# Four seven-product pairs instead of three in eight gate and up blocks, with the lo parts of three chunks per block made by an adding DMA

## The chip, the cores and the metric

The kernel runs on one NeuronCore of a Trainium2 chip. The metric is the device time of one execution, in microseconds (us). Before the change it is 1479.21 us, the median of three runs (1479.01 to 1479.62).

## The reference

One decoder layer on 256 tokens of width 2048, float32: a mixer, an attention over 256 memory tokens, a SwiGLU feed-forward part of width 5632, each behind an RMSNorm and added to the residual, and a last RMSNorm.

```python
h = x
h = h + hybrid_mixer(rmsnorm(h, norm_mix), w_in, ..., w_out)
h = h + memory_cross_attention(rmsnorm(h, norm_xa), mem_n, w_q, w_k, w_v, w_o)
h = h + swiglu(rmsnorm(h, norm_ffn), w_gate, w_up, w_down)
return rmsnorm(h, norm_final)

def swiglu(h, w_gate, w_up, w_down):
    return (jax.nn.silu(h @ w_gate) * (h @ w_up)) @ w_down
```

The change touches the two products `h @ w_gate` and `h @ w_up`.

## The kernel before, in words

**Chunks.** All weights stream from memory once, in one order (stream_plan). A chunk is 256 rows by 512 columns of a weight, held as one raw tile `r` of 128 partitions by 1024 elements (512 KB). SyncE (SP) issues the loads (load_to, L192 to L201) into six raw buffers, some five chunks ahead. The order of the work of TensorE (PE) and of SP is that in which the code is written (manual_schedule); the framework's scheduler orders VectorE (DVE), ScalarE (ACT) and GpSimd (POOL), and an engine runs its instructions strictly in that order.

**Hi and lo parts.** A float32 product is made of three products of a shorter format: hi with hi, lo with hi, hi with lo. split_to (L224) makes a chunk's hi part `h` by a cast on ACT (L238) and its lo part `l = r - h` on DVE (L239); there are four buffers for each. The activations are split in the same way beforehand. tok_mm (L303) multiplies a plain chunk by both halves of the tokens: eight matmuls with `h` (L312 hi, L313 lo of the activations), then four with `l` (L316), twelve in all.

**Gate and up blocks.** The feed-forward part goes by blocks n = 0 to 10 of 512 columns. In a block the chunks are (g,n,c) of the gate and (u,n,c) of the up weight, c = 0 to 7; below, g4 or u7 is c = 4 or 7 of the block that is spoken of. A gate and an up chunk of the same c may be made a pair (Strassen's method in Winograd's form, over two token halves and the two weights): 21 matmuls by seven_mm (L980; L990 and L991 with hi parts, L993 with lo parts) instead of the 24 of two plain chunks. A pair needs sums of its two chunks: pair_sums (L207) adds four times on DVE (L213 to L216), casts three sums on ACT (L220) and makes their lo parts on DVE (L221). The sums' parts lie in "slots" (63 buffers of 128 by 512). The matching sums of the activations come from token_sums (L954), once for each c. SEVEN (L31) says how many pairs each block has: three in blocks 1 to 9, two in block 10, none in block 0. Within a block with three pairs the order is pair 0, g3 g4 u3, pair 1, g5 u4 g6, pair 2, g7 u5 u6 u7.

**After a block.** What the pairs share is added up by p_post (L934, L938 to L942). `whole` (L1227, L1232) adds it to the accumulators of gate and up, on DVE, once the last matmul of these has run; g_post makes the silu (ACT, L1241), u_post the product (DVE, L1249). The result is transposed (DVE, L331), written to memory (SP, put, L344) and read back (SP, get, L351) in the layout for the down product, and split (L1259, L1260).

**Order around a block's start.** When the last matmul of u7 has run, PE goes on with pair 0 of the next block at once. DVE then has the old block's two `whole` of up (L1232), two L1249, two transposes, and then lo parts and the sums of the new block's pair 1. unit (L380) runs up to two parts after another, asks for loads up to AHEAD (6) chunks on and for splits one to three chunks on. A load waits until its raw buffer's last reader is done.

## Time and profile before

| | |
|---|---|
| median of three runs | 1479.21 us (1479.01 to 1479.62) |
| the profiled execution | 1479.07 us |
| its span in the profile | 1477.3 us |
| granted TensorE clock, mean | 0.999 |
| busy: PE, DVE, ACT, POOL | 1466.2, 1212.1, 864.2, 34.6 us |
| moved by DMA | 350.91 MB, mean 238 GB/s |

A profile is one execution, read by an engine's rows: the line of the program, the operation, the tiles written and read (`out<-in`, buffer numbers left out), the count, busy time and mean time of one in ns, and idle time of the engine ahead of the group with what ended it. Times of single instructions are microseconds from the start of the span. Instructions of an engine overlap a little, so that the step from one start to the next is shorter than the duration of one. The time of a run is about 1.8 us more than the span.

### The profile page before, as it was taken

The numbers are of one execution on the slowest core, as the hardware profiler recorded it, in microseconds if no ns is written. First come the engines' busy times: TensorE is split into PE (matmuls) and PEld (weight loads), VectorE is DVE, ScalarE is ACT, GpSimd is POOL, SyncE is SP. The second block draws the span as 40 slices with busy tenths as digits, with TensorE's granted clock in tenths as the row PEclk, the third lists the DMA queues.
The fourth block names the chain that finished last, engine by engine and source line by source line (L and its number), as shares of the span: only waits on it lengthen the run. The fifth ranks groups of instructions, "written<-read, shape, count | busy, mean of one in ns | idle before, by whom it ended". The sixth has DMA issues, their size and how long they took to land.

```text
span 1477.3 us, 18842 instructions
## 1 busy us (share of the span) xinstructions
PE 1466.2 (99%) x6592; PEld 1208.1 (82%) x6592; DVE 1212.1 (82%) x1738; ACT 864.2 (58%) x1228; POOL 34.6 (2%) x46
## 2 busy tenths in 40 slices
PE   9999999999999999999999999999999999999997
PEld 7788888888888888888888888888888887888886
DVE  6667777876786775897578999999999998979995
ACT  7467654866664544665466665556655554655663
POOL 0012000101000000000000000000000000000000
PEclk9999999999999999999999999999999999999999
DMA  9877766868667675777658766656676666765553
GB/s 367 273 252 260 264 220 228 289 219 307 228 240 267 198 249 186 254 271 278 226 172 296 263 217 230 214 212 228 229 248 248 206 237 229 269 219 199 195 202 112
DMA packets 151519, 350.91 MB, mean 238 GB/s; under 512 B 11616, under 2 KB 63232, under 8 KB 151424
## 3 DMA queue, kind: packets, MB, share of 16 engines
q1 hardware_dynamic: 142368, 342.83, 66.6%
q10 hardware_dynamic: 9056, 6.87, 1.6%
q8 instruction: 51, 0.84, 0.2%
q14 instruction: 44, 0.36, 0.1%
HBM read 323.40 MB, written 26.26 MB: 237 GB/s over the span
## 4 chain that ended last, share of the span: by engine, by line
PE 98%; DVE 1%; issue 0%; DMA 0%; ACT 0%; DVEq 0%; POOLq 0%; POOL 0%; SPq 0%
PE a L312 27%; PE a L313 26%; PE a L316 26%; PE m L993 3%; PE m L990 3%; PE m L991 3%; PE a L991 2%; PE a L990 2%; PE a L993 2%; PE m L733 1%; PE m L312 0%; PE m L313 0%; PE m L316 0%; PE m L1147 0%; PE m L735 0%
## 5 line engine op out<-in xcount | busy, mean ns | idle before, releaser
L238 ACT CAST h<-r 128x1024 fp32r<-128x1024 f32 (+1 forms) x539 | 562.5, 1048 | 405.2 <-PE a L313 231.8
L239 DVE TENSOR_TENSOR l<-r,h 128x1024 fp32r<-128x1024 f32 (+1 forms) x539 | 650.5, 1216 | 175.0 <-ACT h L238 166.5
L312 PE MATMUL a<-h,s 128*128 128x512 f32 x1735 | 679.3, 392 | 0.1
L313 PE MATMUL a<-h,s 128*128 128x512 f32 x1735 | 675.6, 389 | 0.0
L316 PE MATMUL a<-l,s 128*128 128x512 f32 x1735 | 466.9, 389 | 0.0
L312 PEld LDWEIGHTS a<-h,s 128*128 128x128 f32 x1735 | 326.0, 188 | 69.5 <-issue 2.0
L316 PEld LDWEIGHTS a<-l,s 128*128 128x128 f32 x1735 | 325.6, 188 | 68.1 <-DVE l L239 0.4
L313 PEld LDWEIGHTS a<-h,s 128*128 128x128 f32 x1735 | 326.0, 188 | 66.8
L220 ACT CAST s<-b 128x512 fp32r<-128x512 f32 x94 | 58.0, 618 | 60.9 <-DVE b L213 55.6
L221 DVE TENSOR_TENSOR s<-b,s 128x512 fp32r<-128x512 f32 x94 | 64.6, 687 | 0.1
L331 DVE STREAM_TRANSPOSE b<-s 128x512 f32<-128x512 f32 x62 | 40.7, 690 | 7.0 <-ACT s L338 7.0
L213 DVE TENSOR_TENSOR b<-r,r 128x512 f32<-128x512 f32 x47 | 32.2, 686 | 7.8 <-DMA r<-in_w_dram 7.8
L674 DVE SCALAR_TENSOR_TENSOR t<-t,vec,t 128x255 f32<-128x255 f32 (+2 forms) x72 | 33.0, 489 | 5.8 <-ACT t L671 5.1
L214 DVE TENSOR_TENSOR r<-r 128x512 f32<-128x512 f32 x47 | 32.4, 689 | 0.7
L216 DVE TENSOR_TENSOR r<-b,r 128x512 f32<-128x512 f32 x47 | 32.2, 686 | 0.1
L221 DVE TENSOR_TENSOR s<-r,s 128x512 fp32r<-128x512 f32 x47 | 32.2, 685 | 0.0
L215 DVE TENSOR_TENSOR b<-b,r 128x512 f32<-128x512 f32 x47 | 32.2, 685 | 0.0
L220 ACT CAST s<-r 128x512 fp32r<-128x512 f32 x47 | 29.0, 618 | 4.6 <-DVE r L216 3.2
L993 PE MATMUL m<-s,t 128*128 128x512 f32 x76 | 29.6, 389 | 0.0
L990 PE MATMUL m<-s,t 128*128 128x512 f32 x76 | 29.6, 389 | 0.0
L991 PE MATMUL m<-s,t 128*128 128x512 f32 x76 | 29.6, 389 | 0.0
L338 ACT ACTIVATE s<-a,xr 128x512 f32<-128x512 f32 x42 | 26.5, 681 | 4.2 <-issue 3.7
(240 smaller groups left out, 1241.4 us busy)
## 6 DMA issues: line engine op xcount, KB each, us to landing
r<-in_w_dram SPq DMA_DIRECT2D x535, 512.0 KB, 4.8
w<-b SPq DMA_DIRECT2D x42, 512.0 KB, 3.3
f<-w SPq DMA_DIRECT2D x42, 512.0 KB, 4.9
s<-acsT ACTq DMA_DIRECT2D x24, 256.0 KB, 5.1
s<-in_xt_dram SPq DMA_DIRECT2D x16, 256.0 KB, 7.0
s<-in_mt_dram SPq DMA_DIRECT2D x8, 256.0 KB, 6.3
s<-in_m_dram SPq DMA_DIRECT2D x8, 256.0 KB, 6.1
parked<-s SPq DMA_DIRECT2D x8, 256.0 KB, 8.4
```

The source lines that it names most:

```text
L220: nc.scalar.copy(h, x)
L221: tt(l, x, h.bitcast(F32), ALU.subtract)
L238: nc.scalar.copy(h[:, c], r[:, c])
L239: tt(l[:, c], r[:, c], h[:, c].bitcast(F32), ALU.subtract)
L312: mm(ps[tb], ah, h[:, w], start=first and i == ks[0], stop=False)
L313: mm(ps[tb], al, h[:, w], start=False, stop=False)
L316: mm(ps[tb], blocks(i, tb)[0], l[:, i * 512:i * 512 + 512], start=False, stop=stop and i == ks[-1])
L331: nc.vector.transpose(t[:, tb * 512:tb * 512 + 512], src[tb])
L674: stt(a[:, d:], u[:, 0:T - d], v("cw", 4 * ct + k), a[:, d:], ALU.mult, ALU.add)
L990: mm(ps, ah, bh, start=any(ps is q for q in start), stop=False)
L991: mm(ps, al, bh, start=False, stop=False)
L993: mm(ps, ah, bl, start=False, stop=any(ps is q for q in stop))
```

## The change

Blocks 1 to 8 get four pairs, block 9 keeps three, block 10 two. The order in a block with four is pair 0, g4, pair 1, g5 u4, pair 2, g6 u5, pair 3, g7 u6, u7.

For 24 chunks (BY_DMA: g4, u4 and u5 of blocks 1 to 8) DVE makes no lo part. ACT casts the hi part (L241 of the changed kernel) and writes its negative into the lo tile (L242, `l = -h`), and a DMA issued by POOL adds the raw chunk to it in place (L243, `l = l + r`). The lo matmuls of such a chunk are kept back ("late") and run behind the next part: those of g4 behind pair 1, for instance. There are five lo buffers instead of four and 61 slots instead of 63. The first sum's two parts of a gate and up pair go to the pool of the gate tiles (four buffers) instead of slots. token_sums runs for four c instead of three, for c = 2 and 3 in the wide form.

Line numbers of the changed kernel: loads L201, pair sums L215 to L218, their casts and lo parts L225 and L226, a chunk's hi and lo L247 and L248, plain matmuls L321, L322 (hi) and L327 (lo), seven_mm L1013, L1014 (hi) and L1016 (lo), `whole` L1255, silu L1264, the product L1272, transposes L348, write and read back L361 and L368.

```diff
-SEVEN = {n: 3 if n < 10 else 2 for n in range(1, 11)}
+SEVEN = {n: 4 if n < 9 else 3 if n < 10 else 2 for n in range(1, 11)}
+BY_DMA = {(m, n, c) for n in range(1, 9) for m, c in (("g", 4), ("u", 4), ("u", 5))}
...
-                    3: ("g3 g4 u3", "g5 u4 g6", "g7 u5 u6 u7")}[SEVEN[n]]
+                    3: ("g3 g4 u3", "g5 u4 g6", "g7 u5 u6 u7"),
+                    4: ("g4", "g5 u4", "g6 u5", "g7 u6 u7")}[SEVEN[n]]
...
-        lop = E(tc.tile_pool(name="lo", bufs=4))
-        sp = E(tc.tile_pool(name="slots", bufs=63))
+        lop = E(tc.tile_pool(name="lo", bufs=5))
+        sp = E(tc.tile_pool(name="slots", bufs=61))
...
-                h, l = slot(dt=F32R), slot(dt=F32R)
+                if key[0] in "gu" and not pair_parts[key]:
+                    h, l = [gtp.tile([128, 512], F32R, tag="g", name=nm("g")) for _ in range(2)]
+                else:
+                    h, l = slot(dt=F32R), slot(dt=F32R)
...
-                m = 2 if i in (0, 2) else 1
+                if key in BY_DMA:
+                    nc.scalar.copy(h, r)
+                    act(l, h.bitcast(F32), AF.Identity, scale=-1.0)
+                    nc.gpsimd.dma_start(l.bitcast(F32), r, accum_op=ALU.add)
+                m = 0 if key in BY_DMA else 2 if i in (0, 2) else 1
...
-            for i in ks:
-                for tb in tbs:
-                    mm(ps[tb], blocks(i, tb)[0], l[:, i * 512:i * 512 + 512], start=False, stop=stop and i == ks[-1])
+
+            def lo_part():
+                for i in ks:
+                    for tb in tbs:
+                        mm(ps[tb], blocks(i, tb)[0], l[:, i * 512:i * 512 + 512], start=False,
+                           stop=stop and i == ks[-1])
+
+            if key in BY_DMA:
+                late.append(lo_part)
+            else:
+                lo_part()
...
             for i, (ks, fn) in enumerate(parts):
+                left = late[:]
                 fn()
+                for f in left:
+                    f()
+                    late.remove(f)
...
-                for c in range(3):
-                    token_sums(c, [(h2g[2 * c + k][:, 0:T], h2g[2 * c + k][:, T:]) for k in range(2)], c == 2)
+                for c in range(4):
+                    token_sums(c, [(h2g[2 * c + k][:, 0:T], h2g[2 * c + k][:, T:]) for k in range(2)], c > 1)
```

What moves, at three places. The first is DVE at a block's start, from the old block's transposes on, before. `b` of the transposes is their output; `l` is a lo part, `r` a raw chunk, `h` its hi part; `b` and `s` of the lines behind are a pair's sums and their lo parts.

```order
L331 STREAM_TRANSPOSE b_8271<-g_8191 128x512
L331 STREAM_TRANSPOSE b_8271<-g_8194 128x512
L239 TENSOR_TENSOR l_8279<-r_8177,h_8278 128x1024
L239 TENSOR_TENSOR l_8301<-r_8234,h_8300 128x1024
L239 TENSOR_TENSOR l_8305<-r_8244,h_8304 128x1024
L213 TENSOR_TENSOR b_8336<-r_8244,r_8282 128x512
L214 TENSOR_TENSOR r_8282<-r_8282 128x512
L215 TENSOR_TENSOR b_8336<-b_8336,r_8282 128x512
L221 TENSOR_TENSOR s_8342<-b_8336,s_8341 128x512
L216 TENSOR_TENSOR r_8244<-b_8336,r_8244 128x512
L221 TENSOR_TENSOR s_8346<-b_8336,s_8345 128x512
L239 TENSOR_TENSOR l_8354<-r_8282,h_8353 128x1024
```

The same place after the change, where `g` takes the first sum's lo part:

```order
L348 STREAM_TRANSPOSE b_8316<-g_8252 128x512
L348 STREAM_TRANSPOSE b_8316<-g_8255 128x512
L248 TENSOR_TENSOR l_8325<-r_8238,h_8324 128x1024
L215 TENSOR_TENSOR b_8340<-r_8238,r_8279 128x512
L216 TENSOR_TENSOR r_8279<-r_8279 128x512
L217 TENSOR_TENSOR b_8340<-b_8340,r_8279 128x512
L226 TENSOR_TENSOR g_8346<-b_8340,g_8345 128x512
L218 TENSOR_TENSOR r_8238<-b_8340,r_8238 128x512
L226 TENSOR_TENSOR s_8350<-b_8340,s_8349 128x512
L248 TENSOR_TENSOR l_8358<-r_8279,h_8357 128x1024
```

Two of the three lo parts ahead of pair 1's sums are gone; the last row of each is the lo part of u1. The second place is PE ahead of pair 1 in a block: before, the lo matmuls of the last plain chunk stand there, with 57 matmuls of the block ahead of pair 1 (`m` and `a` are accumulators).

```order
L316 MATMUL a1983_8978<-l1999_9041,s1547_7133 128x512
L316 MATMUL a1984_8979<-l1999_9041,s1547_7133 128x512
L990 MATMUL m1985_8980<-h2000_9044,s1505_6966 128x512
L991 MATMUL m1985_8980<-h2000_9044,s1505_6966 128x512
L990 MATMUL a1981_8976<-h2000_9044,s1506_6969 128x512
L991 MATMUL a1981_8976<-h2000_9044,s1506_6969 128x512
L993 MATMUL m1985_8980<-l2001_9045,s1505_6966 128x512
L993 MATMUL a1981_8976<-l2001_9045,s1506_6969 128x512
L990 MATMUL m1988_8983<-h2011_9093,t1586_7297 128x512
```

After, PE comes to pair 1 from the hi matmuls of g4, with 29 matmuls of the block ahead of it; the last row is the first that reads the lo part of u1.

```order
L322 MATMUL a2013_9056<-h2022_9093,s1572_7256 128x512
L1013 MATMUL m2016_9059<-h2024_9098,s1505_6966 128x512
L1014 MATMUL m2016_9059<-h2024_9098,s1505_6966 128x512
L1013 MATMUL a2012_9055<-h2024_9098,s1506_6969 128x512
L1014 MATMUL a2012_9055<-h2024_9098,s1506_6969 128x512
L1016 MATMUL m2016_9059<-l2025_9099,s1505_6966 128x512
L1016 MATMUL a2012_9055<-l2025_9099,s1506_6969 128x512
L1013 MATMUL m2019_9062<-h2035_9131,t1586_7297 128x512
L1014 MATMUL m2019_9062<-h2035_9131,t1587_7298 128x512
L1013 MATMUL m2017_9060<-g2029_9119,t1584_7293 128x512
L1014 MATMUL m2017_9060<-g2029_9119,t1585_7294 128x512
L1016 MATMUL m2019_9062<-l2036_9132,t1586_7297 128x512
```

The third place is SP behind the write of a finished block's result, before. The loads are of the chunks to come; a name in brackets is what the load waits for: DMAHW are earlier DMAs, DVE and Activation the readers of the raw buffer.

```order
L344 DMA w1997_9038<-b1990_9011 128x2x512 [waits DVE_49]
L199 DMA r2002_9060<-in_w_dram 128x1024 [waits DMAHW6_49]
L351 DMA f2003_9074<-w1997_9038 128x8x128 [waits DMAHW4_49]
L199 DMA r2013_9097<-in_w_dram 128x1024 [waits DMAHW7_49,DVE_49]
L199 DMA r2014_9099<-in_w_dram 128x1024 [waits DMAHW0_49,DVE_49]
```

After, DMASW stands for an adding DMA of POOL:

```order
L361 DMA w2027_9112<-b2021_9090 128x2x512 [waits DVE_49]
L201 DMA r2037_9135<-in_w_dram 128x1024 [waits DMAHW4_49,Activation_49]
L201 DMA r2038_9137<-in_w_dram 128x1024 [waits DMAHW6_49,DMASW4_49]
L368 DMA f2039_9164<-w2027_9112 128x8x128 [waits DMAHW3_49]
L201 DMA r2044_9175<-in_w_dram 128x1024 [waits DMAHW0_49,DMAHW7_49,DVE_49,Activation_49]
L201 DMA r2045_9177<-in_w_dram 128x1024 [waits DVE_49]
L201 DMA r2061_9232<-in_w_dram 128x1024 [waits DMAHW1_49,DVE_49]
L201 DMA r2062_9234<-in_w_dram 128x1024 [waits DMAHW2_49,DMASW5_49,Activation_49]
```

The two loads with DMASW are those of u2, which takes over the buffer of g4, and of u3, which takes over that of u4: they now stand behind the adding DMA on the old chunk, and what is queued on SP behind them waits as well.

More of the change, by code (lines that the diff above doesn't have):

```diff
@@ L378, in trunk @@
         AHEAD = 6
+        late = []
         def unit(parts, post=None):
```

## The prediction, made before the changed kernel was run

> **What bounds the kernel now.** I read the profile's page first: busy shares and the chain that ended last.
>
> ```profile
> PE 1466.2 (99%) x6592; PEld 1208.1 (82%) x6592; DVE 1212.1 (82%) x1738; ACT 864.2 (58%) x1228; POOL 34.6 (2%) x46
> ...
> PE 98%; DVE 1%; issue 0%; DMA 0%; ACT 0%; DVEq 0%; POOLq 0%; POOL 0%; SPq 0%
> ```
>
> TensorE (PE) is the whole story of the sum: a matmul that goes is time that goes, and a wait of PE is time that comes. But DVE's 82% is an average over stages, so next come the windows of the stage that changes, one per gate and up block. Where a block begins is read from the PE timeline: the first matmul of a block's first pair is a row of L990 with a new accumulator.
>
> ```profile
> 863.70 0.39 PE L990 MATMUL m<-h,s 128*128 128x512 f32 x1
> 905.18 0.39 PE L990 MATMUL m<-h,s 128*128 128x512 f32 x1
> ```
>
> The same rows fall every 41.48 us through blocks 2 to 8. The windows' columns are: stretch, its length, then busy us and instructions of PE, PE's weight loads, DVE, ACT, POOL, then granted clock, DMA share, GB/s.
>
> ```profile
> 863.70:905.18 41.48, 41.48 (x185) 34.35 (x183) 39.60 (x51) 24.32 (x31) 0.00 (x0) 1.00 0.64 225
> 905.18:946.66 41.48, 41.48 (x185) 34.35 (x183) 39.97 (x52) 24.30 (x31) 0.00 (x0) 1.00 0.64 229
> ...
> sum 290.36, PE 290.36 PEld 240.43 DVE 278.97 ACT 169.88 POOL 0.00; mean PE 41.48 PEld 34.35 DVE 39.85 ACT 24.27 POOL 0.00
> ```
>
> PE never stops here, but DVE has 39.85 of 41.48 us filled: two engines are nearly even. The clock is 1.00 throughout. A block has 183 matmuls (3 pairs of 21, 10 plain chunks of 12), so one costs 41.48/183 = 0.2267 us.
>
> **The matmuls removed.** A pair takes 21 where two plain chunks take 24. One more pair in each of eight blocks removes 24: 24 x 0.2267 = -5.44 us. A block of 180 takes 40.80 us.
>
> **DVE's own load.** I need the spacing of its instructions, from the timeline of DVE at a block's start (start, us, ..., how many in a row):
>
> ```profile
> 863.67 1.29 DVE L1232 TENSOR_TENSOR f<-a,f 128x512 f32<-128x512 f32 x2
> 864.88 1.41 DVE L1249 SCALAR_TENSOR_TENSOR g<-f,fscale,g 128x512 f32<-128x512 f32 x2
> 866.20 1.30 DVE L331 STREAM_TRANSPOSE b<-g 128x512 f32<-128x512 f32 x2
> 867.42 3.45 DVE L239 TENSOR_TENSOR l<-r,h 128x1024 fp32r<-128x1024 f32 x3
> 870.79 0.69 DVE L213 TENSOR_TENSOR b<-r,r 128x512 f32<-128x512 f32 x1
> 871.51 0.69 DVE L214 TENSOR_TENSOR r<-r 128x512 f32<-128x512 f32 x1
> 872.12 0.68 DVE L215 TENSOR_TENSOR b<-b,r 128x512 f32<-128x512 f32 x1
> 872.72 0.69 DVE L221 TENSOR_TENSOR s<-b,s 128x512 fp32r<-128x512 f32 x1
> 873.33 0.69 DVE L216 TENSOR_TENSOR r<-b,r 128x512 f32<-128x512 f32 x1
> 873.98 0.69 DVE L221 TENSOR_TENSOR s<-b,s 128x512 fp32r<-128x512 f32 x1
> 874.59 1.22 DVE L239 TENSOR_TENSOR l<-r,h 128x1024 fp32r<-128x1024 f32 x1
> ```
>
> Back to back, a 512-wide instruction takes 0.61 us (872.12 to 872.72) and a 1024-wide one 1.12 ((870.79 - 867.42)/3). A block loses three lo parts (-3.36) and gains seven instructions of a pair's sums (4 L213 to L216, 3 L221: +4.27): 39.85 + 0.91 = 40.76, against PE's 40.80. No throughput is short by itself, but nothing is left to catch up with.
>
> **ACT's load**, from the groups of this stage (busy, mean ns | idle before):
>
> ```profile
> L239 DVE TENSOR_TENSOR l<-r,h 128x1024 fp32r<-128x1024 f32 x112 | 135.2, 1217 | 9.2 <-ACT h L238 9.1
> L238 ACT CAST h<-r 128x1024 fp32r<-128x1024 f32 x113 | 119.1, 1054 | 86.7 <-issue 28.0 <-PE a L991 27.0 <-PE a L313 10.5
> L220 ACT CAST s<-b 128x512 fp32r<-128x512 f32 x42 | 25.9, 618 | 34.0 <-DVE b L213 33.9
> L1241 ACT ACTIVATE g<-f,fscale 128x512 f32<-128x512 f32 x14 | 9.3, 714 | 0.0
> ```
>
> Three more 0.62 us casts, and three 1024-wide negations, which no row shows: between a cast's 1.05 and twice 0.714, I take 1.15 (1.05 plus what an ACTIVATE of 512 takes over a CAST, 0.10). 24.27 + 1.86 + 3.45 = 29.6 of 40.8: hidden as load, though not as latency, below. Pair 3's token sums are built once more, in unit 8 (before block 1), where DVE is idle 4.46 of 42.00 us. Four adds of 128 columns, two of 256 and one 512-wide lo part are 4 x 0.28 + 2 x 0.42 + 0.69 = 2.7: hidden.
>
> ```profile
> 768.00:810.00 42.00, 42.00 (x187) 34.74 (x186) 37.54 (x69) 26.90 (x48) 0.80 (x1) 1.00 0.83 273
> ...
> L960 DVE TENSOR_TENSOR f<-s 128x256 f32<-128x256 f32 x6 | 2.5, 417 | 0.0
> L962 DVE TENSOR_TENSOR f<-f 128x128 f32<-128x128 f32 x3 | 0.9, 285 | 0.0
> ```
>
> **First wait: pair 1's lo part.** At a block's start DVE must finish the old block: two L1232 (they need the last matmul of the old up accumulators), two L1249, two transposes, then lo parts and pair 1's sums, in that order. In the rows the lo part of u1 is done at 874.59 + 1.22 = 875.81, 12.1 us after the block's start at 863.70. PE wants it late:
>
> ```profile
> 878.89 0.39 PE L993 MATMUL m<-l,t 128*128 128x512 f32 x1
> ```
>
> That is 15.2 us in, after 67 matmuls (pair 0's 21, g3 g4 u3, 10 of pair 1): 3.1 us to spare. After the change one lo part instead of three stands ahead of the sums: 12.1 - 2 x 1.12 = 9.9 us. But PE reaches it after pair 0, g4's eight hi matmuls and 10 of pair 1: 39 x 0.2267 = 8.84. So PE stops about 1.0 us. The wait recurs, as the chain starts anew from each block's last matmul: blocks 2 to 8, 7 times, +7.1 (block 1 has no L1232 of a block before it, 1.25 us less; block 9 keeps the order of three pairs). This alone eats the 5.44.
>
> **Second wait: the loop through the adding DMA.** A chunk whose lo part comes by DMA holds its raw buffer until that has landed, and SP's loads wait for buffers in order. Let M be the time from the end of the negation to the landing. From whole(u), L1232, at 0: six instructions 3.75 (863.67 to 867.42), one lo part 1.12, L213 to L214 1.33: at 6.2 ACT may cast u1. ACT's order is then u1, a sum, g5, a sum, u4, g2, u4's negation. Its spacings:
>
> ```profile
> 872.37 1.06 ACT L238 CAST h<-r 128x1024 fp32r<-128x1024 f32 x1 [0.24 <-DVE r L214]
> 873.32 0.62 ACT L220 CAST s<-b 128x512 fp32r<-128x512 f32 x1
> 873.85 1.05 ACT L238 CAST h<-r 128x1024 fp32r<-128x1024 f32 x1
> ```
>
> 0.95 for a chunk, 0.53 for a sum: 6.2 + 4 x 0.95 + 2 x 0.53 + 1.15 = 12.2, with a little for hand-overs 12.4. The load of u3 waits for that DMA and takes 4.5 to land; then DVE does pair 3's sums, and from there to the next whole(u) it has 27 instructions, 20 of 512 and 7 of 1024: 20 x 0.61 + 7 x 1.12 = 20.0. The loop takes 12.4 + M + 4.5 + 20.0 = 36.9 + M, say 37.0 with u3's own hand-over. It is slower than PE with the first wait (41.8) from M = 4.8 on.
>
> ```profile
> r<-in_w_dram SPq DMA_DIRECT2D x112, 512.0 KB, 4.5
> w<-b SPq DMA_DIRECT2D x7, 512.0 KB, 3.0
> ...
> parked<-s SPq DMA_DIRECT2D x8, 256.0 KB, 8.4
> ...
> GB/s 367 273 252 260 264 220 228 289 219 307 228 240 267 198 249 186 254 271 278 226 172 296 263 217 230 214 212 228 229 248 248 206 237 229 269 219 199 195 202 112
> ```
>
> No adding DMA and no DMA of POOL is in the trace. Its bounds: 3.0, a plain transfer of 512 KB out of SBUF, and 8.4, the slowest row here. I take 4.5, the landing of 512 KB in SBUF, plus a second 512 KB that must be read to be added to, 0.52 MB at the page's best 367 GB/s = 1.4: M = 5.9, so the loop is 42.9. The Trainium skill, "DMA: Bandwidth & Descriptors", section "Anatomy of one DMA — SWDGE (gpsimd) path", gives 2.0 us plus bytes over 436 GB/s for a transfer that GpSimd issues, an estimate of 3.2 for this size, and by that the loop (40.2) would not bind and the time would be 1480.7; no run here shows it, and it is for plain copies.
>
> Block 2 stops 1.9 (its whole(u) comes 42.9 - 1.25 - 40.8 = 0.85 late, plus 1.0), blocks 3 to 8 stop 42.9 - 40.8 = 2.1 each: 1.9 + 6 x 2.1 = 14.5, the first wait included. The other queues: u2's load waits for g4's DMA, but DVE comes to u2 late enough up to M about 7; SP's two small transfers behind it (L344's write, then L351's read) have about 7 us. The DMA engines stand at 0.64 and move about 17% more bytes (1.6 MB onto 225 GB/s x 41.48 = 9.3 MB): no bound. The slots that go and the gate tiles that hold pair sums cost nothing that I can find in these orders.
>
> **Sum**, against the profiled execution's 1479.07 (the median is 1479.21, the same): 1479.07 - 5.44 + 14.5 = 1488.1; on the median **1488**.
>
> **Rivals.** A measurement of this kernel can tell 0.2% (3.0 us) from no change.
>
> *The DMA is quick* (M under 4.8): only the first wait is left, 1479.1 - 5.4 + 7.1 = 1480.8, within 0.2%. For it: w's 3.0 us. Against: DVE also waits for ACT's casts now, 9.1 us in seven blocks (the L239 row), 1.3 each; with 40.76 busy that gives 42.05 a block and 1482.5. Chance 0.17.
>
> *The DMA is slow or held up*: M = 7.5 (4.5 + 3.0, read and write in sequence) makes the loop 44.5: 3.5 + 6 x 3.7 = 25.7, 1499.3; M = 8.4 makes it 45.4: 4.4 + 6 x 4.6 = 32.0, 1505.6. For it: a kind of transfer without any row, on a POOL that issues nothing in these windows. The Trainium skill, "SBUF — State Buffer", section "Who interferes with whom", warns that such a DMA's descriptors starve while DVE runs in a mode that uses both ports. DVE's rows speak against that mode: 1024 columns take 1217 ns and 512 take 688, the time goes with the width. Chance 0.22.
>
> ```profile
> L221 DVE TENSOR_TENSOR s<-b,s 128x512 fp32r<-128x512 f32 x42 | 28.9, 688 | 0.0
> ```
>
> *No wait shows: faster.* DVE's load (40.76) is under PE's (40.80). If DVE's chain at the block's start is shorter than I count by the 1.0 us that is short, and M under 3.8, the whole 5.44 stays: 1473.7. It takes over 0.6 us off the chain in each of seven blocks to win 3.0 us. For it: no PE wait of this stage in the trace, spare time of 3 us at the present place. Against: the order of DVE is fixed, its rows agree from block to block. Chance 0.09.
>
> **Numbers.** My forecast has 0.52. Faster by over 0.2%: 0.09; within: 0.17; slower: 0.52 + 0.22 = 0.74. The range goes from the quick DMA, 1480.5, to M = 8.4, 1506; outside lie the faster case and a DMA slower than any row.
>
> **What would show it.** Right: PE waits on the lo part of a pair's u chunk, about 2 us a block, in blocks 2 to 8; DVE waiting on a load at the first sum of pair 3; SP waiting on the adding DMA; a block period of 42.9; issue to landing near 5.9. Wrong: a period of 40.8 (neither wait), 41.8 to 42.1 (no loop), or PE stopping at another instruction, such as a late lo matmul of the chunks that come by DMA.

## The result, and the profile after

The changed kernel takes 1519.29 us (median of four runs, 1517.56 to 1522.28), the kernel before 1479.16: a ratio of 1.0273, 95% interval 1.0256 to 1.0289. It is 40 us slower where the prediction had 9. The profiled execution took 1518.92 us, with a span of 1517.2, 39.9 more than before; all numbers below are set against that.

First the page of the changed kernel: busy shares, the DMA queues of SP (q1) and of POOL (q0), the chain that ended last, and the landings.

```profile
PE 1481.3 (98%) x6568; PEld 1210.4 (80%) x6568; DVE 1220.3 (80%) x1777; ACT 897.2 (59%) x1277; POOL 55.1 (4%) x70
...
q1 hardware_dynamic: 142368, 342.83, 65.5%
q0 software_dynamic: 3456, 12.58, 4.3%
...
PE 79%; DVE 11%; DMA 6%; issue 2%; ACT 1%; SPq 0%; POOL 0%; DVEq 0%; POOLq 0%; ACTq 0%
...
r<-in_w_dram SPq DMA_DIRECT2D x535, 512.0 KB, 5.0
...
l<-r POOLq DMA_DIRECT2D x24, 512.0 KB, 7.1
```

PE had 98% of the chain before and has 79% now; DVE and DMA have come into it. Where is read from the windows by block, from block 1 to block 8 (period, PE, its loads, DVE, ACT, POOL, clock, DMA share, GB/s):

```profile
826.03:866.87 40.84, 40.84 (x182) 33.79 (x180) 35.13 (x47) 23.62 (x30) 1.87 (x3) 1.00 0.85 258
866.87:915.92 49.05, 44.84 (x181) 35.32 (x180) 43.93 (x61) 31.43 (x41) 2.59 (x3) 0.93 0.74 225
...
1008.78:1055.91 47.13, 44.20 (x181) 35.62 (x180) 41.82 (x57) 29.61 (x39) 2.58 (x3) 0.93 0.76 234
1055.91:1099.24 43.33, 41.37 (x181) 33.63 (x180) 37.79 (x52) 25.82 (x33) 2.59 (x3) 1.00 0.83 255
...
1148.16:1191.19 43.03, 41.39 (x182) 33.63 (x180) 37.88 (x52) 25.71 (x32) 2.62 (x3) 1.00 0.84 256
```

Block 1 takes 40.84 us, as 180 matmuls should: the gain is there. Blocks 2 to 8 take (1191.19 - 866.87)/7 = 46.33 on average instead of 40.80. Block 0 takes 47.34 us (778.69 to 826.03) instead of 43.52, block 9 44.08 instead of 41.48. The whole: -5.44 for the matmuls, +3.8 in block 0, 7 x 5.53 = +38.7 in blocks 2 to 8, +2.6 in block 9, 39.7 of 39.9.

Where PE stops, from its timeline in block 5 (the first is 8.0 us after the block's start and 35 matmuls into it):

```profile
1018.61 0.50 PE L1013 MATMUL m<-h,t 128*128 128x512 f32 x1 [1.67 <-ACT h L247]
...
1021.07 0.80 PE L1016 MATMUL m<-l,t 128*128 128x512 f32 x1 [1.25 <-DVE l L248]
1021.66 0.63 PE L1016 MATMUL m<-g,t 128*128 128x512 f32 x1
1022.09 0.63 PE L1013 MATMUL m<-s,t 128*128 128x512 f32 x1
```

The stop at u1's lo part is the one that the prediction named. Ahead of it is a stop at u1's hi part, which it did not name, and behind it matmuls come every 0.43 us instead of 0.2267: the clock fell.

The waits of blocks 2 to 8 (who, for whom: us in all, times, longest). The 21 waits of SP are those for the three adding DMAs of each block:

```profile
SPq L201 <- DMA l<-r: 114.1, 21, 9.6
...
DVE b L215 <- DMA r<-in_w_dram: 23.5, 11, 5.6
...
PE m L1016 <- DVE l L248: 9.9, 8, 1.6
PE m L1013 <- ACT h L247: 8.2, 7, 1.7
```

**The loop, in block 5.** From the timeline: the start of whole(u), the negation of u4, the issue of its adding DMA, and DVE from pair 3's first sum to the next whole(u).

```profile
1011.23 1.28 DVE L1255 TENSOR_TENSOR f<-a,f 128x512 f32<-128x512 f32 x2
...
1022.34 1.05 ACT L242 ACTIVATE l<-h 128x1024 fp32r<-128x1024 f32 x1
...
1023.80 0.86 POOL L243 DMA_DIRECT2D l<-r  x1 [11.07 <-ACT l L242]
...
1034.34 0.68 DVE L215 TENSOR_TENSOR b<-r,r 128x512 f32<-128x512 f32 x1
...
1043.42 2.36 DVE L248 TENSOR_TENSOR l<-r,h 128x1024 fp32r<-128x1024 f32 x2 [1.24 <-ACT h L247]
1047.08 0.69 DVE L215 TENSOR_TENSOR b<-r,r 128x512 f32<-128x512 f32 x1 [1.30 <-DMA r<-in_w_dram]
...
1057.31 1.28 DVE L1255 TENSOR_TENSOR f<-a,f 128x512 f32<-128x512 f32 x2
```

And the DMA issues of two stretches of it, at 1023.8 (that adding DMA) and at 1030.56 (the load of u3, which waited for it); the last column is from issue to landing.

```profile
l<-r POOLq DMA_DIRECT2D x1, 512.0 KB, 6.7
...
r<-in_w_dram SPq DMA_DIRECT2D x1, 512.0 KB, 3.5
```

From whole(u) at 1011.23 to the end of the negation at 1023.39 are 12.2 us (forecast 12.4). The DMA has landed at 1023.80 + 6.7 = 1030.5, so M = 7.1 (forecast 5.9). The load behind it lands 3.5 later (4.5), pair 3's sums begin at 1034.34, and from there to the next whole(u) are 23.0 us (20.0): the 27 instructions and 2.5 us of waiting, half of it for the load of the next block's u0 and half for a cast of ACT, which had waited for PE to be done with a hi buffer. 46.1 in all, where the prediction had 42.9.

The other blocks go the same way. The whole(u) of blocks 2 to 8 start at 871.19, 917.09, 964.59, 1011.23, 1057.31, 1103.52 and 1149.24, steps of 45.7 to 47.5 us, though the blocks by PE's first matmul, above, vary from 43.0 to 49.1. M is 7.1 to 9.1 in the seven blocks, 7.8 on average. In block 5 DVE is busy until 1034.34, 0.3 us past the landing of u3's load; in blocks 3 and 6 it stands 5.6 and 2.8 us for that load.

### The profile page after: what moved, and what is told of

Its sections match the earlier page's. It is cut to its first block, busy times and chain, and to the rows that moved or that the text cites. A ratio compares the mean times of both kernels' runs of the same rounds, so it can differ in the third digit from the quotient of the medians.

```text
span 1517.2 us, 18946 instructions
## 1 busy us (share of the span) xinstructions
PE 1481.3 (98%) x6568; PEld 1210.4 (80%) x6568; DVE 1220.3 (80%) x1777; ACT 897.2 (59%) x1277; POOL 55.1 (4%) x70
## 4 chain that ended last, share of the span: by engine, by line
PE 79%; DVE 11%; DMA 6%; issue 2%; ACT 1%; SPq 0%; POOL 0%; DVEq 0%; POOLq 0%; ACTq 0%
PE a L327 22%; PE a L321 22%; PE a L322 21%; DMA r<-in_w_dram 3%; DVE l L248 3%; PE m L1016 2%; DMA l<-r 2%; PE m L1013 2%; PE m L1014 2%; PE a L1013 1%; PE a L1014 1%; PE a L1016 1%; DVE s L226 1%; DVE f L1255 1%; DVE b L215 1%
## 5 line engine op out<-in xcount | busy, mean ns | idle before, releaser
L248 DVE TENSOR_TENSOR l<-r,h 128x1024 fp32r<-128x1024 f32 (+1 forms) x515 | 621.4, 1217 | 173.9 <-ACT h L247 172.9
L247 ACT CAST h<-r 128x1024 fp32r<-128x1024 f32 (+1 forms) x515 | 535.4, 1045 | 347.8 <-PE a L322 238.5
L321 PE MATMUL a<-h,s 128*128 128x512 f32 x1671 | 655.5, 392 | 1.1 <-ACT s L912 1.1
L322 PE MATMUL a<-h,s 128*128 128x512 f32 x1671 | 651.8, 390 | 0.6 <-DVE s L913 0.6
L327 PE MATMUL a<-l,s 128*128 128x512 f32 x1671 | 451.9, 391 | 1.0 <-DVE l L248 1.0
L327 PEld LDWEIGHTS a<-l,s 128*128 128x128 f32 x1671 | 315.8, 189 | 68.0 <-DVE l L248 1.7
L321 PEld LDWEIGHTS a<-h,s 128*128 128x128 f32 x1671 | 314.3, 188 | 68.4 <-issue 1.8
L322 PEld LDWEIGHTS a<-h,s 128*128 128x128 f32 x1671 | 314.5, 188 | 65.4 <-DVE s L913 0.9
L225 ACT CAST s<-b 128x512 fp32r<-128x512 f32 x73 | 45.1, 619 | 42.2 <-DVE b L217 23.5
L215 DVE TENSOR_TENSOR b<-r,r 128x512 f32<-128x512 f32 x55 | 37.8, 687 | 32.7 <-DMA r<-in_w_dram 32.6
L225 ACT CAST g<-b 128x512 fp32r<-128x512 f32 x37 | 22.9, 618 | 59.1 <-DVE b L215 54.1
L226 DVE TENSOR_TENSOR s<-b,s 128x512 fp32r<-128x512 f32 x73 | 50.2, 687 | 6.4 <-ACT s L225 6.4
L348 DVE STREAM_TRANSPOSE b<-s 128x512 f32<-128x512 f32 x62 | 40.7, 690 | 6.5 <-ACT s L355 6.5
L226 DVE TENSOR_TENSOR s<-r,s 128x512 fp32r<-128x512 f32 x55 | 37.8, 687 | 6.3 <-ACT s L225 3.7
L225 ACT CAST s<-r 128x512 fp32r<-128x512 f32 x55 | 34.0, 617 | 11.3 <-DVE r L218 11.1
L218 DVE TENSOR_TENSOR r<-b,r 128x512 f32<-128x512 f32 x55 | 37.7, 686 | 0.0
L243 POOL DMA_DIRECT2D l<-r x24 | 20.9, 871 | 367.2 <-ACT l L242 323.4
L241 ACT CAST h<-r 128x1024 fp32r<-128x1024 f32 x24 | 25.1, 1046 | 9.1 <-issue 8.0
L1016 PE MATMUL m<-l,s 128*128 128x512 f32 x72 | 28.5, 396 | 1.9 <-DVE l L248 1.6
```

The source lines that it names most:

```text
L215: tt(f[:, a], g[:, a], u[:, a], ALU.add)
L225: nc.scalar.copy(h, x)
L226: tt(l, x, h.bitcast(F32), ALU.subtract)
L247: nc.scalar.copy(h[:, c], r[:, c])
L248: tt(l[:, c], r[:, c], h[:, c].bitcast(F32), ALU.subtract)
L321: mm(ps[tb], ah, h[:, w], start=first and i == ks[0], stop=False)
```

## The experiments

Two theories had come out of this. *A*: the adding DMA holds raw buffers, SP's loads stand behind it, DVE is late. *B*: the fourth pair itself, its sums and the place of pair 1, costs it. A third, *C*, came with the shares of the DMA engines: the adding DMA is twice as heavy as its bytes and slows the loads beside it.

### Four pairs without the adding DMA

```diff
-BY_DMA = {(m, n, c) for n in range(1, 9) for m, c in (("g", 4), ("u", 4), ("u", 5))}
+BY_DMA = set()
```

> The changed kernel, but with no chunk by the adding DMA: DVE makes the lo parts of g4, u4 and u5 as it does the others, and their lo matmuls follow at once. Four pairs, the order of the chunks, five lo buffers and 61 slots stay. Theory A (the adding DMA holds raw buffers some 7 us, SP's loads stand behind it in order and come late and in bursts, DVE and ACT come late to a block's start, PE stops there and then runs at a lower clock): DVE then has 40.76 + 3.36 = 44.1 us of work a block against PE's 40.8, so a block takes about 44.1 by DVE's load alone, 8 x 3.3 = 26 above a block without waits: 1479.1 - 5.4 + 26 + 3.8 (token sums, which stay) = 1503.5, plus up to 8 for lower clock, so 1503 to 1512, faster than the changed kernel's 1519.3, and SP's loads never wait on a POOL DMA. Theory B (the fourth pair costs it: its sums on DVE and ACT, and pair 1 so near the block's start; the DMA relieves DVE and its own delay is hidden): slower than the changed kernel, 1519.3 + 8 x 3.36 = 1546, or at least not faster.

1503.14 us, ratio 1.0161 (1.0146 to 1.0177). One of its blocks; the next has the same load (44.16 us):

```profile
910.02:954.63 44.61, 41.71 (x182) 33.48 (x180) 44.15 (x59) 25.21 (x35) 0.00 (x0) 1.00 0.61 212
```

DVE is busy 44.15 us, the 44.1 that was counted, and sets the block. B falls as stated: giving DVE three lo parts more made the kernel 16 us faster. The pair does need those 3.4 us from somewhere, but the adding DMA costs more than it saves.

### The adding DMA with three pairs

```diff
-SEVEN = {n: 4 if n < 9 else 3 if n < 10 else 2 for n in range(1, 11)}
+SEVEN = {n: 3 if n < 10 else 2 for n in range(1, 11)}
...
-                for c in range(4):
-                    token_sums(c, [...], c > 1)
+                for c in range(3):
+                    token_sums(c, [...], c == 2)
```

> The kernel with three pairs in blocks 1 to 9 and the order of before, but with the lo parts of g4, u4 and u5 of blocks 1 to 8 by ACT's negation and the adding DMA, and their lo matmuls one part later. Buffers as in the changed kernel. DVE has 39.85 - 3.36 = 36.5 us of work in a block of 41.5. Theory A (the held raw buffers make loads late): DVE and PE wait on loads here as well, though DVE has 5 us a block to make up for it; some stops of PE of 0 to 2 us a block, 1479 to 1495, SP's waits on the adding DMA above 60 us in all. Theory B (the fourth pair costs it): no stop of PE, 1479.1 within 1 us, although SP waits on the DMA.

1494.04 us, ratio 1.0099 (1.0083 to 1.0116), at the upper end for A. With 3.4 us less work a block DVE is later than before. Its waits for loads in blocks 1 to 8, before and in this kernel:

```profile
DVE b L213 <- DMA r<-in_w_dram: 2.0, 4, 0.9
```

```profile
DVE b L215 <- DMA r<-in_w_dram: 33.3, 9, 6.0
```

The DMA alone costs 15 us, where DVE's work was taken away.

### A plain copy in the place of the adding

```diff
-                    nc.gpsimd.dma_start(l.bitcast(F32), r, accum_op=ALU.add)
+                    nc.gpsimd.dma_start(l.bitcast(F32), r)
```

> The changed kernel, but POOL's DMA copies the raw chunk into the lo tile and adds nothing (the lo parts are then the raw chunks, so what is computed differs); number, size and place of the transfers stay. If it is the adding, a second stream of 512 KB to read, that makes the DMA take 7.1 us: 4 to 5 us from issue to landing and a time of 1500 to 1510. If it is the way a DMA issued by POOL goes, or its meeting with the loads in the DMA engines: 6 to 7 us as before and 1515 to 1520.

1505.31 us, ratio 1.0170 (1.0138 to 1.0203). The shares of POOL's queue in blocks 2 to 8, of the changed kernel (324.3 us) and of this one (312.0 us; packets, MB, share of 16 engines):

```profile
q0 software_dynamic: 3024, 11.01, 17.5%
```

```profile
q0 software_dynamic: 3024, 11.01, 8.7%
...
l<-r POOLq DMA_DIRECT2D x21, 512.0 KB, 6.2
```

The adding doubles what the same bytes take of the DMA engines (17.5% of 324.3 us is 56.8, 8.7% of 312.0 is 27.1). But from issue to landing a plain copy takes 6.2 us where the adding DMA took 7.0. So neither expectation holds whole: the time is that of the first, the landing that of the second, and most of the landing is that of a DMA of POOL among loads. Of the 14 us that the kernel gains (its four runs lie between 1498.02 and 1509.35), 7 x 0.8 = 5.6 would be the shorter loop; that the rest is what the adding takes from the loads is argued here, not shown.

### Seven raw buffers

```diff
-        rawp = E(tc.tile_pool(name="raw", bufs=6))
+        rawp = E(tc.tile_pool(name="raw", bufs=7))
...
-        sp = E(tc.tile_pool(name="slots", bufs=61))
+        sp = E(tc.tile_pool(name="slots", bufs=59))
```

> The changed kernel with seven raw buffers instead of six and 59 slots instead of 61. A load then takes over a buffer that was let go one chunk earlier, about 2.7 us of PE's time at twelve matmuls a chunk, up to 5 at a pair. Theory A (held raw buffers): SP's waits on the adding DMA fall from 131.8 us to under 70, loads come 3 to 5 us earlier, PE's stops at the block's start shrink to the 1.0 us of pair 1's nearness, few stretches of lower clock: 1479.1 - 5.4 + 7 x 1.4 + 3.8 = 1487, up to 1495. Theory B (the fourth pair's sums and its place): 1515 to 1520. Theory C (the DMA engines have too many bytes): the same 1515 to 1520, with landings as long as before.

1531.36 us, ratio 1.0356 (1.0340 to 1.0371): slower, which no theory had. SP's waits for the adding DMA were to fall from 131.8 us to under 70; they are 141.7 between 820 and 1240 us alone, so the seventh buffer did not take the hold away. POOL's transfers land in 7.7 us in blocks 2 to 8 (median), and DVE waits for loads longer than in the changed kernel:

```profile
DVE b L215 <- DMA r<-in_w_dram: 41.5, 7, 8.2
```

Loads that run further ahead may meet the adding DMA in a bunch; that is a guess from the landings. The kernel also has two slots fewer, which wasn't run by itself with four pairs. So this run decides nothing between A and C.

### Token sums later

```diff
-                for c in range(4):
+                for c in range(3):
                     token_sums(c, [(h2g[2 * c + k][:, 0:T], h2g[2 * c + k][:, T:]) for k in range(2)], c > 1)
+            if i == 12:
+                token_sums(3, [(h2g[6 + k][:, 0:T], h2g[6 + k][:, T:]) for k in range(2)], True)
```

> The changed kernel with the token sums of pair 3 built four units later than the other three (unit 12 instead of 8). In the changed kernel's trace PE stops 1.2 and 0.85 us at block 0's chunk whose activations DVE finishes 2.8 us later than before, and then runs 1.7 us behind at a lower clock: block 0 took 47.34 us instead of 43.52. If the token sums in front of that work on DVE are the cause: block 0 takes 43.5 again and the time is 3.8 less, 1515.5. If the stop has another cause (the first loads or slots): block 0 stays at 47 and the time at 1519.

1515.84 us, ratio 1.0253 (1.0229 to 1.0277), 3.5 less. The intervals of the two kernels overlap; what shows it is block 0, which is back at its time:

```profile
778.95:822.47 43.52, 43.52 (x194) 36.04 (x193) 37.34 (x71) 29.55 (x44) 1.70 (x2) 1.00 0.81 286
```

### Pair 1 later

```diff
-                    4: ("g4", "g5 u4", "g6 u5", "g7 u6 u7")}[SEVEN[n]]
+                    4: ("g4 g5", "u4 g6", "u5", "g7 u6 u7")}[SEVEN[n]]
```

> The changed kernel with another order in the blocks of four pairs: pair 0, g4 g5, pair 1, u4 g6, pair 2, u5, pair 3, g7 u6 u7. PE comes to the lo part of u1 after 55 matmuls of a block (12.5 us) instead of 39 (8.84); DVE has it done at about 11.0 by the rows of before. If the nearness of pair 1 to the block's start is what costs (the first wait of the prediction, 1.4 us a block as measured, and the clock that falls with two stops in a row): no stop there, blocks of 41 to 42.5, 1490 to 1498. If the held raw buffers and late loads cost (theory A): DVE is late at the block's start all the same, PE stops at other places (accumulators that wait for L1255, pair 2 or 3), 1505 to 1520.

1516.34 us, ratio 1.0248 (1.0233 to 1.0263): 3 us less, at the edge of what the intervals tell apart. The stops at pair 1 are gone, and PE waits for the adding DMA itself, at lo matmuls that now run behind one plain chunk:

```profile
PE a L327 <- DMA l<-r: 23.5, 12, 4.1
```

The first wait of the prediction is real, but taking it away wins little while the adding DMA is as late.

### The adding DMA reads from memory

```diff
-                    nc.gpsimd.dma_start(l.bitcast(F32), r, accum_op=ALU.add)
+                    nc.gpsimd.dma_start(l, wst[offs[i]:offs[i] + 128 * w].rearrange("(p n) -> p n", p=128).bitcast(F32R), accum_op=ALU.add)
```

> The changed kernel, but the adding DMA reads the chunk again from the weights in memory instead of from the raw buffer. The raw buffer is then free after its cast, as for any chunk, and SP's loads don't stand behind the DMA. The transfer's bytes and its adding stay. Theory A (held raw buffers): SP's waits on the adding DMA go to none, loads come as early as before, DVE is on time; left are the nearness of pair 1 (1.4 us in seven blocks) and the token sums (3.8): 1479.1 - 5.4 + 9.9 + 3.8 = 1487.4, up to 1493. Theory C (the adding DMA takes the DMA engines twice as long as its bytes, 17.5% of them against 8.7% for a plain copy, and slows the loads beside it): loads still land late, 1505 to 1520.

1495.05 us, ratio 1.0101 (1.0084 to 1.0118), 24 less than the changed kernel. No load waits for the adding DMA any more, but landings in blocks 2 to 8 grow:

```profile
r<-in_w_dram SPq DMA_DIRECT2D x112, 512.0 KB, 6.3
l<-in_w_dram POOLq DMA_DIRECT2D x21, 512.0 KB, 9.0
```

Near A's 1487 to 1493 and far from C's 1505: the held buffer is the larger part, and a rest of 2 to 8 us stays, with slow landings (4.5 before). The source of the transfer has changed as well, so the 24 us are not the hold's alone by proof.

### All three, and a better order

The kernel with memory as the source, pair 1 later and the token sums later:

> The last three together: the adding DMA reads from memory, pair 1 later in the block, pair 3's token sums four units later. Theory A: no cause of a stop is left; DVE has 40.76 of 40.80 us a block, so between 1473.7 (nothing lost) and 1483 (DVE's waits for casts, 1.3 us a block as before, come on top). Theory C: 1495 to 1515, with stops of PE in every block.

Ratio 1.0138 (1.0115 to 1.0161), 1495.6 to 1502.95 in three runs (a fourth took 3833.87 and is left out). No faster than the source alone: nearly every stop of blocks 2 to 8 is now at u4's lo matmuls, behind one plain chunk.

```profile
PE a L327 <- DMA l<-in_w_dram: 15.8, 7, 3.6
```

Then the order so that the lo matmuls of g4 and u4 come behind a whole pair, with the weights in memory as source, and with the raw buffer:

```diff
-                    4: ("g4 g5", "u4 g6", "u5", "g7 u6 u7")}[SEVEN[n]]
+                    4: ("g5 g4", "g6 u4", "u5", "g7 u6 u7")}[SEVEN[n]]
```

> As the kernel with all three, but in the order pair 0, g5 g4, pair 1, g6 u4, pair 2, u5, pair 3, g7 u6 u7: the lo matmuls of g4 and u4 now run behind a whole pair (4.8 us) instead of a plain chunk (2.7). In the one before every stop of blocks 2 to 8 was at the lo matmuls of u4, 1.4 to 3.7 us, waiting on the adding DMA, which takes 8.2 us there. PE reaches the lo part of u1 after 51 matmuls, 11.6 us, DVE has it at about 11.0. If the lo matmuls simply came too soon behind their DMA: the stops shrink by the 2.0 us gained, blocks of 40.8 to 42.1, 1474 to 1484. If the adding DMA slows everything that lands beside it (theory C), the stops move to another place and the time stays at 1493 to 1502.

> The kernel above (order, token sums later) with the adding DMA reading the raw buffer, as in the changed kernel. What it takes longer than the kernel above is the price of the held raw buffers alone. Theory A: 15 to 25 us more than that kernel, SP's waits on the adding DMA near 100 us in all. If the order was the whole cause: within 3 us of it.

1485.94 us, ratio 1.0039 (1.0024 to 1.0054), from memory; 1497.07, ratio 1.0113 (1.0095 to 1.0131), from the raw buffer. The hold, with the change of source, is worth 11 us in this order, between the two expectations; SP waits for the adding DMA as it did:

```profile
SPq L201 <- DMA l<-r: 86.2, 21, 9.3
```

In the better of the two DVE hardly waits for loads, and PE's stops at the lo parts of pairs' u chunks are 3.7 us in all:

```profile
DVE b L215 <- DMA r<-in_w_dram: 6.0, 6, 1.7
```

It is still 6 us behind the kernel before, in blocks of 41.1 to 43.5.

### PE busy where it stood

```diff
+                near = part[0][0] == "g" and part[0][2] == 1 and 2 <= part[0][1] <= 8 and len(group) == 2 and group[0][0] is p[3]
+                for _ in range(8 if near else 0):
+                    mm(p[0], zero, gh[:, a], start=False, stop=False)
                 for ps, (ah, al), (bh, bl) in group:
...
+                for _ in range(6 if near else 0):
+                    mm(p[0], zero, gh[:, a], start=False, stop=False)
                 for ps, (ah, al), (bh, bl) in group:
```

> The changed kernel with 14 matmuls by a zero matrix (they add zero to an accumulator of the pair) in each of blocks 2 to 8: 8 (1.8 us) ahead of the second group of pair 1 and 6 (1.4 us) ahead of its lo matmuls, where PE stops 1.84 and 1.43 us in most blocks. PE is then busy where it stood. If the lower clock behind these stops comes from the stops: no matmuls at 0.43 us each behind pair 1, and 10 to 12 us less than the changed kernel, 1507 to 1510. If the clock falls for another reason, or if the rows at 0.43 us are waits: the time is the same or up to 10 us more (in blocks that stopped for less than 3.2 us), 1519 to 1529.

1523.60 us, ratio 1.0297 (1.0281 to 1.0312). Block 5, to be set beside its row above:

```profile
1006.52:1053.63 47.11, 45.36 (x195) 35.88 (x194) 41.10 (x56) 28.65 (x37) 2.58 (x3) 1.00 0.76 233
```

The stops did cause the lower clock: it is 1.00 here, where it was 0.93. But the block takes 47.11 us instead of 47.13. What is late now is told by DVE's waits for loads in blocks 2 to 8, two in each block, for the load of u3 and for that of the next block's u0 (23.5 us in the changed kernel):

```profile
DVE b L215 <- DMA r<-in_w_dram: 37.9, 14, 5.0
```

I had counted some 12 us of slow matmuls as a cost; they were time in which PE would have waited for the loop. That theory falls, and the loop through the adding DMA stands.

### Lo parts on POOL

```diff
-                    act(l, h.bitcast(F32), AF.Identity, scale=-1.0)
-                    nc.gpsimd.dma_start(l.bitcast(F32), r, accum_op=ALU.add)
+                    nc.gpsimd.tensor_tensor(l, r, h.bitcast(F32), ALU.subtract)
```

> The changed kernel with the lo parts of g4, u4 and u5 made by POOL in one subtraction of 128 by 1024 (no negation on ACT, no DMA). The raw buffer is let go when that is done. By theory A nothing holds the buffers longer than POOL's instruction takes; if that is 3 us or less and leaves DVE alone, 1485 to 1492 (pair 1's nearness and the token sums remain). If POOL and DVE get in each other's way, DVE's rows become longer while POOL works, and with DVE full at 40.76 us a block every us of that is lost: three subtractions of 2 to 3 us a block, 8 x 6 to 9 us, 1525 to 1560. The Trainium skill, page SBUF — State Buffer, section Who interferes with whom, says that one port pair is shared by GpSimd and VectorE and locked for a whole instruction; by that rule the second.

1522.42 us, ratio 1.0294 (1.0277 to 1.0311).

```profile
L242 POOL TENSOR_TENSOR l<-r,h 128x1024 fp32r<-128x1024 f32 x21 | 90.4, 4305 | 239.8 <-DVE s L226 152.8 <-ACT h L241 87.0
L226 DVE TENSOR_TENSOR g<-b,g 128x512 fp32r<-128x512 f32 x28 | 34.5, 1231 | 0.0
```

The same instructions once more, with shortest, median and longest time in ns:

```profile
L226 DVE TENSOR_TENSOR g<-b,g x28: 674/684/2890, 867.0 to 1181.3; 128x512 fp32r<-128x512 f32 x28
```

POOL takes 4.3 us, more than the 2 to 3 expected. DVE's mean of 1231 ns (687 in the changed kernel) is made by seven rows of 2859 to 2890 ns; the other 21 take 685 or less. So single instructions of DVE are held up, by up to 2.2 us, and the others not at all. The rule of the Trainium skill (SBUF — State Buffer, Who interferes with whom) agrees with this row. The time is a little under the forecast range.

### Is it DVE's load, or the chain at the block's start?

Three kernels on the better one: pair 1 after 63 matmuls, order `("g5 g6 g4", "u4", "u5", "g7 u6 u7")`; g5 by DMA as well; and u6 by DMA with `("g5 g6 g4", "u4", "u5", "u6 g7 u7")`.

> As the kernel with the adding DMA from memory and the order g5 g4, but with the order pair 0, g5 g6 g4, pair 1, u4, pair 2, u5, pair 3, g7 u6 u7. PE reaches the lo part of u1 after 63 matmuls of a block, 14.3 us; DVE has one lo part more ahead of it, 12.1 by the rows of before, 2.2 us to spare. If the chain at the block's start is what holds the kernel before it (0.9 us there and 0.7 at g5's lo part in most blocks): blocks of 40.8 to 41.2, 1474 to 1477, faster than before. If DVE's load is (40.76 busy and its waits for casts, about 1.3 us a block): blocks of 42 still, 1482 to 1486, the stops at other places.

> As the kernel with the adding DMA from memory and the order g5 g4, with g5 by the adding DMA too, four chunks a block. DVE's load falls by 1.12 to 39.64 us of 40.8; PE reaches the lo part of u1 after 47 matmuls, 10.65 us, DVE has it at 9.9. If DVE's load holds the kernel: blocks of 40.8 to 41.2, 1474 to 1477. If the adding DMA's length does (8.6 us there, and g5's lo matmuls come only eight matmuls after its hi ones; the DMA engines get a third more of these transfers): stops at the lo matmuls of g5, 1 to 3 us a block, 1482 to 1500.

> Pair 1 after g5 g6 g4 as in the first of these, and u6 as a fourth chunk by the adding DMA, in the order pair 3, u6 g7 u7, its lo matmuls behind g7. DVE's load 39.64 us, 2.2 us to spare at pair 1. If load or chain or both hold the kernel: 1473.7 to 1476, the full gain of the matmuls. If the adding DMA does: stops at the lo matmuls of u4, u5 or u6, 1480 to 1500.

1500.92 (1.0145, 1.0131 to 1.0159), 1503.28 (1.0162, 1.0145 to 1.0180) and 1503.10 (1.0162, 1.0149 to 1.0176). All three are 15 to 17 us slower than the kernel that they were to mend, and outside every time that was expected. With less for DVE to do, or with more time at the block's start, the kernel was no faster; but the order and the number of transfers changed as well, so what holds the better kernel isn't shown. In the first of them DVE waits for loads again:

```profile
DVE b L215 <- DMA r<-in_w_dram: 21.9, 7, 4.3
```

Which meeting of loads and adding DMAs makes the difference between these four kernels stays open.

### The transfers alone

The kernel before, three pairs, all lo parts on DVE, with 24 adding DMAs that nobody needs. First between two tiles of their own, then with the raw chunk as source:

```diff
+                if key in BY_DMA:
+                    nc.gpsimd.tensor_copy(tick, h[:, 0:1].bitcast(F32))
+                    nc.gpsimd.dma_start(sums, zeros, accum_op=ALU.add)
```

> The kernel before, unchanged in what it computes, with 24 extra adding DMAs of 512 KB between two tiles of their own, issued by POOL when g4, u4 and u5 of blocks 1 to 8 have been cast; nothing waits for them and they hold no buffer (59 slots instead of 63 make room). Theory A (the held raw buffer): no effect, 1479.4 within 1.5 us. Theory C (the transfers slow the loads beside them): r's landing grows from 4.5 to 5 us or more, DVE and PE wait on loads, 1482 to 1495.

> As the run above, but the extra adding DMA takes the raw chunk as its source, so that it holds the raw buffer until it has landed (61 slots). Its result is still used by nobody, and DVE makes all lo parts as before. What it takes longer than the run above is the hold alone. Theory A: 1488 to 1496 (the kernel with three pairs and lo parts by DMA took 1494.0 with less work on DVE). Theory C: the same as the run above within 2 us.

The first took 1559.17 us, ratio 1.0533 (1.0515 to 1.0550), and doesn't answer the question: nothing tied the DMAs to the blocks, and the framework's order of POOL put all 24 at the start of the kernel. Its blocks 1 to 8, without transfers, take 41.48 us each, so that 59 slots cost nothing there. The second took 1489.01, ratio 1.0061 (1.0046 to 1.0076). Then the first again, with each DMA tied to its chunk:

```diff
-                    nc.gpsimd.tensor_copy(tick, h[:, 0:1].bitcast(F32))
+                    nc.gpsimd.tensor_copy(zeros[:, 0:1], h[:, 0:1].bitcast(F32))
```

> The kernel before with 24 extra adding DMAs of 512 KB between two tiles of their own, each tied to the cast of g4, u4 or u5 of blocks 1 to 8 by one column that POOL copies from it; they hold no raw buffer and nothing waits for them (59 slots instead of 63). The run whose transfers read the raw buffer took 1489.0. Theory A (the hold): 1479.4 within 1.5 us, r's landing near 4.5. Theory C (the transfers beside the loads): 1485 to 1489, r's landing 5.0 us or more.

1491.38 us, ratio 1.0078 (1.0061 to 1.0095), 12 us more than the kernel before. Where they lie is read from blocks 1 to 8 and from what follows them (columns as above), in the kernel before and in this one; the last line is what follows block 8 in the kernel with all 24 transfers at its start:

```profile
822.22:1154.06 331.84, 331.84 (x1466) 274.77 (x1464) 317.60 (x406) 194.57 (x241) 0.00 (x0) 1.00 0.64 227
1154.06:1477.30 323.24, 313.99 (x1387) 259.59 (x1385) 286.85 (x422) 176.83 (x237) 1.10 (x2) 0.99 0.62 211
```

```profile
823.83:1162.16 338.33, 334.12 (x1466) 274.14 (x1464) 313.15 (x402) 189.24 (x239) 50.65 (x48) 1.00 0.83 260
1162.16:1490.70 328.54, 316.99 (x1387) 258.77 (x1385) 289.48 (x426) 176.84 (x239) 1.12 (x2) 0.99 0.59 208
```

```profile
1230.74:1558.10 327.36, 316.46 (x1387) 258.89 (x1385) 286.63 (x422) 175.89 (x237) 1.10 (x2) 0.99 0.59 209
```

Of the 13.4 us between the two profiled executions 6.5 lie in blocks 1 to 8, where the transfers are, 1.6 ahead of them and 5.3 behind. Of these 5.3 the last line has 4.1 without any transfer near: in both of these kernels with 59 slots ACT's casts of pair sums wait there for PE's last reading (3.4 and 3.7 us in all), which they don't with 63, so this is the price of the four slots.

The landings in blocks 1 to 8 of this kernel, with DVE's waits for loads (2.0 us in all before), and the landings of the one before it, with the raw buffer held:

```profile
r<-in_w_dram SPq DMA_DIRECT2D x126, 512.0 KB, 6.0
sums<-zeros POOLq DMA_DIRECT2D x24, 512.0 KB, 9.2
...
DVE b L214 <- DMA r<-in_w_dram: 21.1, 10, 3.0
```

```profile
r<-in_w_dram SPq DMA_DIRECT2D x126, 512.0 KB, 5.4
sums<-r POOLq DMA_DIRECT2D x23, 512.0 KB, 5.4
```

Loads landed in 4.5 us before. Transfers that hold nothing and for which nobody waits cost some 6.5 us in eight blocks. That is C, shown by itself. The run with the raw buffer held takes 340.04 us for the same blocks, 1.7 more; the transfers land sooner there, so the two runs don't give the hold's own price at three pairs. At four pairs the runs with and without the hold are 24 and 11 us apart, as above; that DVE has no time there to make up for a late load fits this, and is argued.

## Why the prediction was wrong

It had the direction and the two places, and a fourth of the size.

- **Matmuls removed, -5.44**: right. Block 1 takes 40.84 us, 40.80 forecast.
- **DVE's load 40.76**: right as a sum, as the run without the DMA shows (44.15 with the three lo parts back, 44.12 by the same rows). ACT's load is not what held it.
- **First wait, 1.0 us a block at u1's lo part**: it is there in blocks 2 to 8, with 1.25 us by the row above. Without it, in another order, only 3 us were won, and PE then stopped at the adding DMA instead.
- **Second wait, the loop of 37.0 + M**: right as a mechanism, wrong in size. This is the step that failed, in two terms. M was taken as 5.9, a landing of 4.5 and 1.4 for the second stream; it is 7.1 in block 5 and 7.8 on average. The larger part of that miss is the 4.5: a plain copy in the same place took 6.2 from issue to landing, the adding 0.8 more (7.0 in the median), and 0.4 lie between the negation's end and the issue. And "from there to the next whole(u) it has 27 instructions" left out what those wait for: the load of the next block's g0 stands behind the adding DMA of u5 just as u3's stands behind that of u4, and the load of u0, for which DVE waits, is queued behind g0's. The prediction listed u2's load and left this one out; nor did it count the casts that wait for PE. 20.0 became 23.0. Only the load behind the DMA was quicker than counted (3.5 for 4.5).
- **"No bound" for the DMA engines at 0.64 and 17% more bytes**: wrong. Counted by bytes the transfers add 17% of 0.64 x 41.48, 4.5 us of the engines' time a block; they took 17.5% of 46.33, 8.1 us. The share rose to 0.72 to 0.84 in blocks 2 to 8, and the transfers slow the loads beside them long before the engines are full: 6.5 us in eight blocks at three pairs with nothing held. This was put aside in one clause.
- **Token sums hidden by 4.46 us of idle DVE**: wrong, +3.5 as undone. The idle time of the window was not where it was needed: DVE made the sums ahead of activations for which PE was about to ask, and began these at 807.65 us (804.84 before).
- **The rivals**: the slow DMA (M of 7.5 to 8.4) had M right, 7.8 on average, yet M alone gives 1499 to 1506. The quick DMA and the rival without waits were wrong. The range ended at 1506 because only M was left open in it; the other terms of the loop had no upper end.

Of 31 us that were missed, 24 lie in blocks 2 to 8 (7 x (46.3 - 42.9)), 3.8 in block 0, 2.6 in block 9, which starts with a late DVE. No version tried beats the kernel before; the nearest, 1485.94, is 6 us behind.

## What to carry to other kernels

Where two engines are both full to within a per cent, an added transfer is not free because its queue is empty: count its share of the DMA engines as measured, ask which loads it meets, and which buffers it keeps. A loop through a transfer has to be walked all the way round, with the loads that each of its waits holds back, before its period is compared with the bound. And an idle share in a window covers new work only if the idle time stands where that work has to be done.

## What the runs showed of the hardware

A DMA that adds took twice the engines' time of one that copies: 17.5% of 324.3 us against 8.7% of 312.0 for the same 11.01 MB. Issued by POOL among loads, 512 KB took 6.2 us as a copy and 7.0 with the adding. The Trainium skill (DMA: Bandwidth & Descriptors, Anatomy of one DMA — SWDGE (gpsimd) path) gives 3.2 us for a copy of that size by its fit; no run here had the engines to itself, and beside loads it does not hold. DVE's rows did not grow beside these DMAs:

```profile
L248 DVE TENSOR_TENSOR l<-r,h 128x1024 fp32r<-128x1024 f32 x91 | 109.5, 1217 | 4.3 <-ACT h L247 4.3
```

That is blocks 2 to 8 of the changed kernel, 1217 ns as before, so nothing here shows that DVE and these DMAs hinder each other.

PE's clock fell after two short stops: 1.67 and 1.25 us with four matmuls between them, then some five us at 0.43 us a matmul (block 5: 0.93). In block 4 stops of 1.68 and 0.71 did the same; 0.69 and 1.27 in block 6, and a single 1.61 in block 3, left it at 1.00. The Trainium skill (TensorE: Matmul & The Clock Gate, HAM oscillation — how this bites in real kernels) speaks of idle gaps above about 3.4 us; here no single gap was as long as 2 us, and the measurement decides.
